# A two-layer decoder trunk on one core: four low parts moved to VectorE, one PSUM tile under another tag, one square root earlier in GpSimd's queue

## The chip, the core and the metric

The kernel runs on one core of a Trainium2 chip. The core has a matrix engine (TensorE; PE in the profile, with its weight loads as PEld), a vector engine (VectorE, DVE), a scalar engine (ScalarE, ACT), a general engine (GpSimd, POOL) and a queue that issues transfers (SyncE, SP). Each engine works through its own queue in order, and waits at an instruction whose inputs are not there. The metric is the time of one execution on the device in microseconds (us); lower is better. A profile is one further execution, recorded by the hardware profiler.

## What is computed

The reference takes x (512 positions by 1024 features, float32) through two layers. Cut to what matters:

```
for l in range(2):
    h = rms_norm(x, norm_mix_g[l])
    proj = h @ w_in[l]                 # attention | short convolution | RWKV-7
    ...
    x = x + mixed @ w_out[l]
    h = rms_norm(x, norm_mlp_g[l])
    x = x + square(relu(h @ w_mlp_up[l])) @ w_mlp_down[l]
return rms_norm(x, final_norm_g)
```

The change touches the last two lines of the loop, the MLP: 1024 features go up to 4096 and down again to 1024.

## The kernel before

Everything is kept transposed: a tile has 128 features on the partitions and the 512 positions along the row. x is eight such tiles (`x[0]` to `x[7]`). Each matrix product is made in near-full float32 precision from three passes. Every operand is split into a high part, which is its cast to a reduced format (made by ACT), and a low part, which is the operand less the high part (one subtraction on DVE or POOL). PE then adds up high by high, high by low and low by high. In the profile the parts of a weight are `whi` and `wlo`, those of a middle tile (a squared tile of the MLP) `mh` and `ml`, and those of the normalised input `ahif` and `alof`.

One layer has two stages.

- The **mixing stage** runs from the norm to the output projection, and also makes the first three of the MLP's up products (`NUP = 3`). Its order is written out by hand: the string `ORDER[l]` names work generators by letter, a number repeats a step, and `drive` (L225) takes the next step of each generator in that order. So the string sets the order of each engine's queue. The letters that matter here are d (loads), w (casts of a weight), x and y (low parts of a weight, x on DVE, y on POOL), m (one matmul of a product) and N (the steps of the MLP's norm).
- The norm before the MLP (`inner_norm`, L755) has five N steps: the sums of squares on PE (`pssf`), a scaling on DVE (`rsx`, L365), the inverse square root as a power on POOL (`rrf`, L369), its broadcast by PE (`prbf`), and a copy to `rs` by ACT (`rsf`, L771). In the last line of `ORDER[1]` the first N stands early. The scaling, the root and the broadcast follow at the end, with four m between them, and one y ahead of them.
- The **MLP stage** (from L1377) has no such string: the framework orders its instructions, and so they do not stand on an engine in the order of the code. `up(i)` finishes middle tile i for i from 0 to 3: `square` (L1397) multiplies the relu of the product by `rs` on DVE (L1402) and squares it on ACT (L1404); `kept` (L1388) makes the two parts, the high part on ACT (L1393), the low part on POOL (L1394). The other 28 middle tiles come in 14 pairs (`two`, L1451), each from seven products of 256 columns (`pa`, `pb`, `pc`, weights `shi_p` and `slo_p`). These use blocks that `by_gain` and `blocks` make on ACT and DVE beforehand (`bn`, `t`, `thi`, `tlo`).
- `down(h, js)` (L1521) multiplies four middle tiles by four of the eight output tiles and adds each to `x[j]` on DVE (L1540). The first call, `down(0, range(4))`, is special: outputs 0 and 1 are open at once, each with middle tiles 0 to 2 first, and then each with middle tile 3; their additions are L1535. Outputs 2 and 3 follow.

PSUM has eight banks here: four under the tag `rp`, two under `mm`, two under `at`. A tag's banks are used in turn, and a bank can be written again when its last reader is done. Outputs of `down` use `mm`. In the MLP stage `at` holds only `pc`. The first two up products stand in `mm`, the third and the fourth in `rp`.

Of the kernel before, what the change touches and what calls it, by code (L numbers as in the profile page):

```python
# [10 lines left out]
F32 = mybir.dt.float32  # L11
# [5 lines left out]
ALU = mybir.AluOpType  # L17
# [85 lines left out]

SLOTS = (
         "cp/rk 010 "
# [163 lines left out]
def tile_trunk(ctx: ExitStack, tc: tile.TileContext, xT, wts, prm_d, cst_d, lora_d, gup_d, lam_d, fin_d, out):  # L269
    nc = tc.nc  # L270
    act, dve, pool = nc.scalar, nc.vector, nc.gpsimd
# [27 lines left out]
    def psum(tag, bufs, name):  # L299
        return ps.tile([P, 512], F32, tag=tag, bufs=bufs, name=name)  # L300
# [4 lines left out]
    x = [cp.tile([P, S], F32, tag=f"x{j}", name=f"x{j}") for j in range(NK)]  # L305
# [23 lines left out]
    def weights(g, k0=0, k1=NK, home=None):  # L329

        for a in range(k0, k1, 4):
            n = min(4, k1 - a)
            turn[0] += 1
            if home is None and spare[0] and turn[0] % (WB + 1) == 0:
                pool_, tags, bufs = spare[0], ("raw4", "whi4", "wlo4"), 1
            else:
                pool_, tags, bufs = wp, ("raw", "whi", "wlo"), WB
            raw = pool_.tile([P, 4, P], F32, tag=tags[0], bufs=bufs, name=f"raw{g}_{a}")
            nc.sync.dma_start(raw[:, :n].rearrange("p k c -> p (k c)"), wts[g, :, a * P:(a + n) * P])
            if home is None:  # L340
                hi, lo = [pool_.tile([P, 4, P], F32R, tag=t, bufs=bufs, name=f"w{p}{g}_{a}") for p, t in zip(("hi", "lo"), tags[1:])]
            else:
                hi, lo = home(a)
            act.copy(hi[:, :n], raw[:, :n])  # L344
            (pool if a and lean[0] else dve).tensor_tensor(lo[:, :n], raw[:, :n], hi[:, :n].bitcast(F32), ALU.subtract)  # L345
            for k in range(n):
                yield hi[:, k], lo[:, k]
# [9 lines left out]
    def mm3(out_ps, w, acts, n=NK):  # L357
        for _ in mm3_steps(out_ps, w, acts, n):
            pass
# [12 lines left out]
    def norm_tile(j, key):  # L372

        if j == 0:
            acc = wp.tile([P, S], F32, tag="acc", bufs=1, name=f"acc{key}")
            nrm[key] = [acc]
            act.activation(acc, x[j], AF.Square)
        else:
            sq = wp.tile([P, S], F32, tag="sq", bufs=2, name=f"sq{key}_{j}")
            act.activation(sq, x[j], AF.Square)  # L380
            dve.tensor_tensor(nrm[key][0], nrm[key][0], sq, ALU.add)
# [187 lines left out]
    for l in range(L):  # L569
# [809 lines left out]
        with ExitStack() as mx:  # L1379
# [8 lines left out]
            def kept(m):  # L1388

                i = len(mids)  # L1390
                hi = fp.tile([P, S], F32R, tag="mh", bufs=RING, name=f"mh{l}_{i}")
                lo = fp.tile([P, S], F32R, tag="ml", bufs=RING, name=f"ml{l}_{i}")
                act.copy(hi, m)  # L1393
                pool.tensor_tensor(lo, m, hi.bitcast(F32), ALU.subtract)  # L1394
                mids.append((hi, lo))

            def square(cs, name):  # L1397

                r = fp.tile([P, S], F32, tag="r", bufs=2, name=f"r{name}")
                for i, c in enumerate(cs):  # L1400
                    q = slice(i * H, i * H + c.shape[1])
                    dve.scalar_tensor_tensor(r[:, q], c, 0.0, rs[:, q], ALU.max, ALU.mult)  # L1402
                m = fp.tile([P, S], F32, tag="m", bufs=3, name=f"m{name}")
                act.activation(m, r, AF.Square)  # L1404
                kept(m)
# [115 lines left out]
            def down(h, js):  # L1521

                g, k0 = h // 2, 4 * (h % 2)
                if h == 0 and js[0] == 0:
                    pts = [psum("mm", 2, f"dn{l}_{h}_{j}") for j in js[:2]]
                    ws = [list(weights(wbase + NG_IN + NG_OUT + NG_UP + 8 * g + j, k0, k0 + 4)) for j in js[:2]]
                    for a, b in ((0, 3), (3, 4)):
                        for j, pt, w in zip(js, pts, ws):
                            for k in range(a, b):
                                (whi, wlo), (ahi, alo) = w[k], mids[k]  # L1530
                                pe.matmul(pt, whi, ahi, start=(k == 0), stop=False)
                                pe.matmul(pt, whi, alo, start=False, stop=False)
                                pe.matmul(pt, wlo, ahi, start=False, stop=(k == 3))
                    for j, pt in zip(js, pts):
                        dve.tensor_tensor(x[j], pt, x[j], ALU.add)  # L1535
                    js = js[2:]
                for j in js:
                    pt = psum("mm", 2, f"dn{l}_{h}_{j}")
                    mm3(pt, weights(wbase + NG_IN + NG_OUT + NG_UP + 8 * g + j, k0, k0 + 4), mids[4 * h:4 * h + 4], 4)
                    dve.tensor_tensor(x[j], pt, x[j], ALU.add)  # L1540
                    if h == 2 * N_KG - 1 and j < NK - LATE:
                        norm_tile(j, f"m{l + 1}")
# [4 lines left out]
            for j in range(NK):  # L1547
                by_gain(j)
            down(0, range(4))
            for q in range(4):  # L1550
                blocks(q)
            h, half = 0, 1
            for p in range(N_TWO):
                two(N_ONE + p, N_ONE + N_TWO + p)
                if len(mids) >= 4 * h + 6 and h < 2 * N_KG - 2 * (l == L - 1):
                    down(h, range(4 * half, 4 * half + 4))
                    h, half = h + half, 1 - half
            while h < 2 * N_KG - 2 * (l == L - 1):
                down(h, range(4 * half, 4 * half + 4))
                h, half = h + half, 1 - half  # L1560
# [70 lines left out]
```

## Time and profile before

| | us |
|---|---|
| median of 3 runs | 1250.81 (1249.91 to 1251.99) |
| the profiled execution's own time | 1245.9 |
| its span, first to last instruction | 1244.1 |
| first middle tile's multiplication by rs (L1402) starts, layer 0 | at 290.31 |
| the same, layer 1 | at 901.73 |

The profile gives for each engine the time in which it was busy, lists the instructions in order of time with the idle time before each and what ended it, and sums up who waited for whom. The matrix engine's granted clock was 0.998 of full speed over the span. A time such as 307.22 is counted from the span's start.

### The profile page before, as it was taken

How to read it: one execution, taken by the hardware profiler on the slowest of the kernel's cores; microseconds unless marked ns; L12 is line 12 of the kernel's file. 1: busy time of each engine (PE TensorE's matmuls, PEld its weight loads, DVE VectorE, ACT ScalarE, POOL GpSimd, SP SyncE). 2: the span in 40 equal slices, each digit the busy share in tenths (PEclk: the TensorE clock that was granted, in tenths of full speed). 3: DMA queues.
4: the chain of work that ended last, by engine and by line, in shares of the span. 5: the costliest groups of instructions: out<-in, count | busy, mean ns of one | idle time of the engine just before them, and what ended most of it. 6: DMA issues, size and time to landing. Idle time of an engine off the chain costs nothing.

```text
span 1244.1 us, 25538 instructions
## 1 busy us (share of the span) xinstructions
PE 1228.2 (99%) x9716; PEld 1055.9 (85%) x9716; DVE 931.8 (75%) x1796; ACT 693.0 (56%) x1462; POOL 363.6 (29%) x457
## 2 busy tenths in 40 slices
PE   9999999999999999999999999999999999999997
PEld 6788788887899898989888888888779999998987
DVE  6787888869887676765666777887798867676753
ACT  6785655648455454544465657564675545454552
POOL 1264637343121112120035455463221211111111
PEclk9999999999999999999999999999999999999999
DMA  6523333142432333321235233332433333323121
GB/s 216 164 90 95 113 88 110 52 161 77 136 102 94 106 99 102 100 87 44 68 105 164 82 118 117 94 83 75 150 104 109 107 105 95 109 94 105 57 69 68
DMA packets 84698, 127.94 MB, mean 103 GB/s; under 512 B 21472, under 2 KB 25568, under 8 KB 84576
## 3 DMA queue, kind: packets, MB, share of 16 engines
q1 hardware_dynamic: 83568, 125.64, 32.7%
q8 instruction: 76, 1.25, 0.4%
q10 hardware_dynamic: 1008, 0.68, 0.2%
q14 instruction: 46, 0.38, 0.1%
HBM read 117.11 MB, written 9.18 MB: 102 GB/s over the span
## 4 chain that ended last, share of the span: by engine, by line
PE 93%; DVE 3%; ACT 2%; DMA 1%; issue 1%; POOL 0%; POOLq 0%; SPq 0%; ACTq 0%; DVEq 0%
PE dn L282 24%; PE pj L282 22%; PE pa L282 13%; PE po L282 8%; PE pb L282 7%; PE dnF L282 4%; PE pc L282 3%; PE up L282 3%; PE sc L282 1%; PE ptt L287 1%; PE pg L282 1%; PE pyy L282 1%; DVE tlo L1449 1%; PE pzw L282 1%; PE pst L282 1%
## 5 line engine op out<-in xcount | busy, mean ns | idle before, releaser
L1394 POOL TENSOR_TENSOR ml<-m,mh 128x512 fp32r<-128x512 f32 x64 | 104.5, 1649 | 489.1 <-ACT mh L1393 348.0
L282 PE MATMUL dn<-mh,whi 128*128 128x512 f32 x448 | 175.8, 392 | 2.1 <-DVE x L1535 2.1
L282 PE MATMUL dn<-ml,whi 128*128 128x512 f32 x448 | 175.3, 391 | 2.0 <-POOL ml L1394 2.0
L282 PE MATMUL dn<-mh,wlo 128*128 128x512 f32 x448 | 175.2, 391 | 0.0
L683 POOL TENSOR_TENSOR wlo<-raw,whi 128x512 fp32r<-128x512 f32 x84 | 111.2, 1324 | 211.5 <-ACT whi L671 169.6
L344 ACT CAST whi<-raw 128x512 fp32r<-128x512 f32 x126 | 77.7, 618 | 157.9 <-PE dn L282 148.1
L282 PE MATMUL pj<-ahim,whi 128*128 128x512 f32 x392 | 156.7, 400 | 0.4 <-DVE vf L1280 0.4
L282 PE MATMUL pj<-ahim,wlo 128*128 128x512 f32 x392 | 156.4, 399 | 0.0
L282 PE MATMUL pj<-alom,whi 128*128 128x512 f32 x392 | 155.9, 398 | 0.0
L1540 DVE TENSOR_TENSOR x<-dn,x 128x512 f32<-128x512 f32 x108 | 74.5, 690 | 91.5 <-PE dn L282 91.3
L671 ACT CAST whi<-raw 128x512 fp32r<-128x512 f32 x142 | 87.7, 617 | 76.4 <-PE pj L282 28.9
L1463 ACT CAST shi_p<-s 128x512 fp32r<-128x512 f32 x112 | 69.5, 621 | 79.6 <-PE pa L282 62.3
L345 DVE TENSOR_TENSOR wlo<-raw,whi 128x512 fp32r<-128x512 f32 x126 | 100.2, 797 | 10.2 <-ACT whi L344 7.4
L282 PEld LDWEIGHTS dn<-ml,whi 128*128 128x128 f32 x448 | 84.2, 188 | 19.8 <-POOL ml L1394 2.8
L282 PEld LDWEIGHTS dn<-mh,whi 128*128 128x128 f32 x448 | 84.1, 188 | 20.0 <-DVE x L1535 2.5
L282 PEld LDWEIGHTS dn<-mh,wlo 128*128 128x128 f32 x448 | 84.2, 188 | 18.5
L282 PE MATMUL pa<-thi,shi_p 128*128 128x256 f32 x336 | 95.2, 283 | 0.1
L282 PE MATMUL pa<-tlo,shi_p 128*128 128x256 f32 x336 | 94.9, 282 | 0.0
L282 PE MATMUL pa<-thi,slo_p 128*128 128x256 f32 x336 | 94.2, 280 | 0.0
L1464 DVE TENSOR_TENSOR slo_p<-s,shi_p 128x512 fp32r<-128x512 f32 x112 | 77.7, 695 | 21.8 <-ACT shi_p L1463 19.0
L282 PEld LDWEIGHTS pj<-ahim,whi 128*128 128x128 f32 x392 | 73.8, 188 | 14.0 <-issue 0.8
L282 PEld LDWEIGHTS pj<-alom,whi 128*128 128x128 f32 x392 | 73.9, 188 | 13.9 <-issue 0.5
(416 smaller groups left out, 3246.2 us busy)
## 6 DMA issues: line engine op xcount, KB each, us to landing
raw<-wts SPq DMA_DIRECT2D x389, 256.0 KB, 2.6
qs<-dqhi SPq DMA_DIRECT2D x24, 128.0 KB, 3.5
ks<-dkhi SPq DMA_DIRECT2D x24, 128.0 KB, 3.3
x<-xT SPq DMA_DIRECT2D x8, 256.0 KB, 5.9
dqhi<-qhi SPq DMA_DIRECT2D x6, 256.0 KB, 3.6
dqlo<-qlo SPq DMA_DIRECT2D x6, 256.0 KB, 3.6
dkhi<-khi SPq DMA_DIRECT2D x6, 256.0 KB, 3.0
dklo<-klo SPq DMA_DIRECT2D x6, 256.0 KB, 3.4
```

What stands on the lines that cost most here:

```text
L282: ins = nc.tensor.matmul(*a, **k)
L287: ins = nc.tensor.transpose(*a, **k)
L344: act.copy(hi[:, :n], raw[:, :n])
L345: (pool if a and lean[0] else dve).tensor_tensor(lo[:, :n], raw[:, :n], hi[:, :n].bitcast(F32), ALU.subtract)
L671: yield act.copy(hi[:, k0:k1], raw[:, k0:k1])
L683: yield eng.tensor_tensor(lo[:, k0:k1], raw[:, k0:k1], hi[:, k0:k1].bitcast(F32), ALU.subtract)
L1394: pool.tensor_tensor(lo, m, hi.bitcast(F32), ALU.subtract)
L1449: dve.tensor_tensor(lo[:, u], t, hi[:, u].bitcast(F32), ALU.subtract)
L1463: act.copy(hi, src)
L1464: dve.tensor_tensor(lo, src, hi.bitcast(F32), ALU.subtract)
L1540: dve.tensor_tensor(x[j], pt, x[j], ALU.add)
```

## The change

Three edits.

1. In `kept`, the low parts of the middle tiles 0 to 3 are made by DVE, those of the other 28 by POOL as before. This holds for both layers.
2. In the first call of `down`, output 0 gets its PSUM tile under the tag `at`, output 1 under `mm`. Before, both had `mm`. With the turn of the two `mm` banks, output 2 then follows on the bank that output 1 doesn't have, and output 3 on that of output 1.
3. In the last line of `ORDER[1]`, the y (a low part of a weight on POOL) goes behind the scaling and the root, which now stand together (`m4 N2 y m8 N` in place of `y m4 N m4 N m4 N`). The number of matmuls between the first of these steps and the broadcast is the same. Layer 0's string is not changed.

```diff
-... m5 x m w y m4 N m4 N m4 N m2 w y m N m33 ")
+... m5 x m w m4 N2 y m8 N m2 w y m N m33 ")
```

```diff
                 act.copy(hi, m)
-                pool.tensor_tensor(lo, m, hi.bitcast(F32), ALU.subtract)
+                (dve if i < 4 else pool).tensor_tensor(lo, m, hi.bitcast(F32), ALU.subtract)
                 mids.append((hi, lo))
```

```diff
                 if h == 0 and js[0] == 0:
-                    pts = [psum("mm", 2, f"dn{l}_{h}_{j}") for j in js[:2]]
+                    pts = [psum(("at", "mm")[j], 2, f"dn{l}_{h}_{j}") for j in js[:2]]
```

2 rows, old and new, of the table ORDER are left out of this document.

## The prediction

> **What bounds the kernel now.** I read the page's head first, then the list of what TensorE (PE) waits for, then the order of time around each wait.
>
> ```profile
> span 1244.1 us, 25538 instructions
> PE 1228.2 (99%) x9716; PEld 1055.9 (85%) x9716; DVE 931.8 (75%) x1796; ACT 693.0 (56%) x1462; POOL 363.6 (29%) x457
> PE dn L282 <- DVE x L1535: 2.1, 2, 1.2
> PE dn L282 <- POOL ml L1394: 2.0, 2, 1.0
> PE prbf L282 <- POOL rrf L369: 0.6, 1, 0.6
> ```
>
> PE is busy for 99% of the span, so the kernel gets faster only where PE stops waiting. The last three rows are from the list of PE's waits (total us, times, longest). They are the waits which the three edits name: the low part of a middle tile (ml), the addition that empties a down bank (x, L1535), and layer 1's root (rrf). Together 4.7 us. What each costs in the order of time is a little more, because PE restarts slowly (columns: start, us, engine, line):
>
> ```profile
> 307.22 0.39 PE L282 MATMUL dn<-mh,whi 128*128 128x512 f32 x1
> 308.65 0.50 PE L282 MATMUL dn<-ml,whi 128*128 128x512 f32 x1 [1.04 <-POOL ml L1394]
> 308.99 0.40 PE L282 MATMUL dn<-mh,wlo 128*128 128x512 f32 x1
> 309.23 0.39 PE L282 MATMUL dn<-mh,whi 128*128 128x512 f32 x1
> ```
>
> and a little later, for the addition,
>
> ```profile
> 310.51 0.27 PE L282 MATMUL pa<-ahif,slo_p 128*128 128x256 f32 x1
> 311.94 0.50 PE L282 MATMUL dn<-mh,whi 128*128 128x512 f32 x1 [1.16 <-DVE x L1535]
> ```
>
> and the same two in layer 1:
>
> ```profile
> 915.90 0.39 PE L282 MATMUL dn<-mh,whi 128*128 128x512 f32 x1
> 917.20 0.50 PE L282 MATMUL dn<-ml,whi 128*128 128x512 f32 x1 [0.92 <-POOL ml L1394]
> ...
> 921.34 0.28 PE L282 MATMUL pa<-alof,shi_p 128*128 128x256 f32 x1
> 922.60 0.50 PE L282 MATMUL dn<-mh,whi 128*128 128x512 f32 x1 [0.99 <-DVE x L1535]
> ```
>
> A 512-column matmul normally follows the one before by 0.23 us (308.99 to 309.23), a 256-column one by 0.12. Layer 0, first wait: 308.65 - 307.22 = 1.43, less 0.23 is 1.20; the step after it (308.65 to 308.99) takes 0.34, 0.11 too much: **1.31**. The other three restart with the same 0.50 matmul, so I add 0.11 to each. Second wait: 311.94 - 310.51 = 1.43, - 0.12 + 0.11 = **1.42**. Layer 1 in the same way: 1.30 - 0.23 + 0.11 = **1.18** and 1.26 - 0.12 + 0.11 = **1.25**. The root:
>
> ```profile
> 898.95 0.39 PE L282 MATMUL up<-ahif,wlo 128*128 128x512 f32 x1
> 899.91 1.16 PE L282 MATMUL prbf<-cst,rrf 128*128 128x128 f32 x8 [0.57 <-POOL rrf L369]
> ```
>
> 899.91 - 898.95 - 0.23 = 0.73, and I put the restart at 0.10 here too: **0.83**. All five: 1.31 + 1.42 + 1.18 + 1.25 + 0.83 = 5.99 us. That is what there is to win.
>
> **Root ahead of the weight's low part (layer 1).** One instruction changes place in POOL's queue; nothing is added.
>
> ```profile
> 896.22 0.15 DVE L365 TENSOR_SCALAR rsx<-pssf 128x4 f32<-128x4 f32 x1
> ...
> 897.13 1.30 POOL L683 TENSOR_TENSOR wlo<-raw,whi 128x512 fp32r<-128x512 f32 x1 [7.01 <-ACT whi L671]
> 898.39 1.47 POOL L369 TENSOR_TENSOR rrf<-rsx,ones 128x4 f32<-128x4 f32 x1
> ```
>
> The root's input is there at 896.37, and POOL was idle for 7 us before 897.13. With the root first it runs from 896.4 to 897.9; PE asks for it at 899.18. So the 0.83 goes whole (if the power stretches to twice 1.47, it still ends in time). Behind the root waits the weight's low part: it would end near 899.2 instead of 898.43. It belongs to the third up tile, whose first matmul comes 12 matmuls after prbf, near 903. Cost nothing.
>
> **Low parts on DVE.** Per layer four POOL instructions go and four DVE instructions come. A DVE subtraction of this shape takes 0.68 us (299.13 below); two in an unbroken row take 1.27 (311.21), so each needs 0.60 of the queue. In order of time, all three engines, layer 0's low parts 0 and 1:
>
> ```profile
> 294.52 0.84 DVE L345 TENSOR_TENSOR wlo<-raw,whi 128x512 fp32r<-128x512 f32 x1 [1.11 <-ACT whi L344]
> 295.09 1.43 POOL L1394 TENSOR_TENSOR ml<-m,mh 128x512 fp32r<-128x512 f32 x1 [0.27 <-ACT mh L1393]
> 295.57 1.50 DVE L345 TENSOR_TENSOR wlo<-raw,whi 128x512 fp32r<-128x512 f32 x1 [0.20 <-ACT whi L344]
> ...
> 299.13 0.68 DVE L345 TENSOR_TENSOR wlo<-raw,whi 128x512 fp32r<-128x512 f32 x1
> ```
>
> then low parts 2 and 3 and the additions:
>
> ```profile
> 300.98 2.80 POOL L1394 TENSOR_TENSOR ml<-m,mh 128x512 fp32r<-128x512 f32 x1 [4.46 <-ACT mh L1393]
> 302.55 1.77 DVE L1449 TENSOR_TENSOR tlo<-t,thi 128x512 fp32r<-128x512 f32 x1
> ...
> 306.36 0.62 ACT L1393 CAST mh<-m 128x512 fp32r<-128x512 f32 x1
> 306.72 2.16 DVE L1446 TENSOR_TENSOR t<-bn,t 128x256 f32<-128x256 f32 x3
> 307.05 1.54 POOL L1394 TENSOR_TENSOR ml<-m,mh 128x512 fp32r<-128x512 f32 x1 [3.27 <-ACT mh L1393]
> ...
> 311.21 1.27 DVE L1535 TENSOR_TENSOR x<-dn,x 128x512 f32<-128x512 f32 x2
> ```
>
> and layer 1:
>
> ```profile
> 906.75 1.58 DVE L345 TENSOR_TENSOR wlo<-raw,whi 128x512 fp32r<-128x512 f32 x1 [1.86 <-PE up L282]
> ...
> 911.75 1.28 ACT L474 ACT_TABLE_LOAD   x1
> ...
> 913.84 3.31 POOL L1394 TENSOR_TENSOR ml<-m,mh 128x512 fp32r<-128x512 f32 x1 [6.07 <-ACT mh L1393]
> ...
> 916.54 1.16 DVE L345 TENSOR_TENSOR wlo<-raw,whi 128x512 fp32r<-128x512 f32 x1
> 917.76 0.61 ACT L1393 CAST mh<-m 128x512 fp32r<-128x512 f32 x1
> 918.23 2.52 DVE L1446 TENSOR_TENSOR t<-bn,t 128x256 f32<-128x256 f32 x4
> 918.45 1.34 POOL L1394 TENSOR_TENSOR ml<-m,mh 128x512 fp32r<-128x512 f32 x1 [1.30 <-ACT mh L1393]
> ...
> 921.87 1.28 DVE L1535 TENSOR_TENSOR x<-dn,x 128x512 f32<-128x512 f32 x2
> ```
>
> The important thing here is that a POOL low part already costs DVE time. The DVE subtraction of 295.57 takes 1.50 instead of 0.68 and ends at 297.07, 0.55 after POOL's; that of 302.55 takes 1.77 and ends at 304.32, 0.54 after POOL's 303.78. DVE stands still until POOL is done. [...]
>
> Layer 0's stretch where DVE has no gap (busy for 5.00 in the 5 us from 305, last fence of this text): what goes is 1.77 - 0.68 = 1.09, and about 1.1 from the three steps of 306.72 (2.16, where three of 0.41, less the overlap of 0.08, take 1.07); what comes is two low parts, 1.20. DVE is about 1.0 earlier at the x additions. Low parts 0 and 1 fall where DVE has gaps (1.11 before 294.52, 1.86 before 906.75). Layer 1: the four steps of 918.23 lose about 1.1 (2.52 against 1.4) and the weight's low part of 916.54 loses 0.5, less 1.20: 0.4 earlier, and up to 0.8 more because the root lets the stage begin sooner.
>
> What is late next is low part 3. Layer 0: its cast ends at 306.98, DVE at the earliest at 307.7, PE asks at 307.45: 0.3 late plus 0.1 to restart, if nothing upstream moves; the square behind it is 0.5 earlier on DVE (1.09 less one low part), so I take 0.1, bounds 0 and 1.0 (one more DVE instruction ahead of it). Layer 1: without the wait at 917.20, PE asks 13 steps after 915.90, at 918.86; cast end 918.37 plus 0.75 is 919.12; and PE is up to 0.8 further ahead. I take 0.5, bounds 0 and 1.3. Low part 2 there has its cast just before 913.84, so it is ready near 914.6; PE asks at 916.1. How DVE's queue is ordered is not in the trace, since the framework sets it; hence the wide bounds.
>
> **First down output in another bank.** No instruction is added. Output 2 no longer waits for the addition of output 0: of its bank, the other one of the tag mm, the last reader was the square of an up tile, which the low parts 0 and 1 stand behind already. The next dependence is output 3 on the addition of output 1. Layer 0: outputs 0 and 1 end three steps after 309.23, at 309.92, less 1.31 is 308.61, output 2 takes twelve steps (2.73), to 311.34. The two additions end now at 311.21 + 1.27 = 312.48; 1.0 earlier is 311.5: 0.2 late. Layer 1: near 922.4 against 923.15 less 0.4 to 1.2. I take 0.4 for both layers, bounds 0 and 2.2 (no DVE gain). The six pa matmuls that filled the gap run later, the same work.
>
> **The sum.** 5.99 - 0.1 - 0.5 - 0.4 = 5.0 us. The profiled execution took 1245.9 us (span 1244.1 and 1.8 around it): 1240.9. The median of the runs, 1250.81, stands 4.9 above it; I carry the difference over: **1245.8**. With all bounds against it (4.5) 1.5 us are left, with all in favour 6.0; I take 3.0 to 6.0, so 1244.8 to 1247.8, as the forecast's own range. Does the won time last? PE has no other wait to speak of until the end, and DVE catches up:
>
> ```profile
> 305.00:310.00 5.00, 3.96 (x18) 2.89 (x17) 5.00 (x8) 3.28 (x7) 1.54 (x1) 1.00 0.16 52
> ...
> 330.00:335.00 5.00, 5.00 (x23) 4.05 (x22) 3.37 (x5) 0.87 (x2) 3.22 (x2) 1.00 0.42 145
> ```
>
> (PE, weight load, DVE, ACT, POOL busy in 5 us.) From 330 DVE has gaps again, so PE coming 2 to 3 us earlier finds its operands.
>
> **Rivals.** *The waits move* (14%): DVE's queue is what sets these waits, and with the low parts in it the low parts and the additions come just as late. The wait of output 2 turns up at output 3, and low part 3 is late by most of a full wait in both layers: the root and a quarter of the other four are won, 0.83 + 5.16 / 4 = 2.1: 1248.7. For it: DVE has no gap there. Against: the 1.0 worked out above. [...]
>
> *The order differs* (7%): a low part stands in DVE's queue ahead of its cast and holds squares and additions up. Layer 1's low part 2 is the place: ACT puts a table load of 1.28 (911.75) before its cast, which an order made beforehand may not count. A hold costs PE about as much as the load, and then again in what DVE does next; with one such hold in each wait's place, 4 x 1.28 = 5.1, nothing of the 5.0 is left but noise: about 1250.5.
>
> *Slower* (9%): in the pair stage DVE becomes the bound. A new order puts one instruction ahead of the low part (slo_p) that the next product needs, in each of the 28 pairs. At half an instruction, 0.34, it costs 9.5: 1250.8 - 5.0 + 9.5 = 1255.3; it decides from (5.0 + 2.5) / 28 = 0.27 a pair. For it: DVE takes on work. Against: the list of PE's waits has no row for slo_p, and DVE has gaps from 330.
>
> *It doesn't do what it says* (2%): the framework's order on PE and DVE keeps the same matmuls waiting, 1250.8.
>
> **How the numbers follow.** The forecast has 68%. About 0.2%, 2.5 us, is what a measurement of this kernel can tell from no change, so faster ends at 1248.3: the forecast and the better third of the moved waits, 0.68 + 0.04 = 0.72. Slower is the one case, 0.09; the rest is 0.19. The range runs from 1244.0 (all five won, and 0.8 for the spread of the runs) to 1250.0; it leaves out the slower case, no change, and most of the differing order, together 0.16.
>
> **What would show it.** DVE has 8 instructions more, POOL 8 fewer; L1394 on POOL counts 56. PE's wait for rrf is gone. PE's wait for L1535 is gone or stands at output 3 and is below 0.5. A wait for ml names DVE and is below 0.5 a layer. DVE's long subtractions beside POOL (1.50, 1.77) are 0.68. Wrong is it if PE shows a wait for slo_p in the pair stage, or if output 3 waits for a microsecond.

## The result, and the profile after

| | before | after |
|---|---|---|
| median of 6 runs, us | 1250.27 (1248.29 to 1251.99) | 1239.68 (1239.49 to 1240.52) |
| profiled execution, us (its span) | 1245.9 (1244.1) | 1239.57 (1237.8) |

The ratio of the times is 0.9918 (0.9906 to 0.9931): 10.6 us faster, where 5.0 were forecast, and below the range. From one profiled execution to the other it is 6.3 us. The two differences do not agree, and the experiments are about that.

First what the profile of the changed kernel says. The head of its page and the top of the list of PE's waits:

```profile
span 1237.8 us, 25529 instructions
PE 1226.2 (99%) x9716; PEld 1055.3 (85%) x9716; DVE 932.3 (75%) x1804; ACT 692.3 (56%) x1462; POOL 350.2 (28%) x449
```

```profile
PE idle L282 <- DVE zero L394: 1.2, 1, 1.2
PE prbF L282 <- ACT rhiF L509: 0.8, 1, 0.8
```

DVE has its 8 instructions more and POOL its 8 fewer. DVE is busy for only 0.5 us longer (931.8 before), though 8 x 0.68 = 5.4 us of work came to it: its subtractions no longer stand behind POOL's. Beside low parts 0 to 2 of layer 0, where two of them took 1.50 and 1.77 us before, each takes 0.68 or 0.69 now. The list has no row for dn and none for prbf: all five waits that the prediction added up are gone. The order of time in layer 0, at the same place as the prediction's rows:

```profile
306.31 0.69 DVE L1394 TENSOR_TENSOR ml<-m,mh 128x512 fp32r<-128x512 f32 x1
...
307.24 0.40 PE L282 MATMUL dn<-mh,whi 128*128 128x512 f32 x1
...
307.47 0.40 PE L282 MATMUL dn<-ml,whi 128*128 128x512 f32 x1
...
308.40 0.40 PE L282 MATMUL dn<-mh,wlo 128*128 128x512 f32 x1
...
308.52 1.28 DVE L1535 TENSOR_TENSOR x<-dn,x 128x512 f32<-128x512 f32 x2
308.63 0.40 PE L282 MATMUL dn<-mh,whi 128*128 128x512 f32 x1
```

Low part 3 is ready at 307.00, and PE asks for it at 307.47. Output 2 follows on output 1 at the normal step of 0.23 (308.40 to 308.63). The two additions start at 308.52 instead of 311.21. Two stretches of 30 us, layer 0 and layer 1, after and then before (the stretch, then busy time of PE, weight load, DVE, ACT, POOL, then PE's granted clock):

```profile
290.00:320.00 30.00, 30.00 (x157) 25.71 (x156) 28.52 (x52) 21.90 (x41) 1.19 (x1) 1.00 0.32 100
900.00:930.00 30.00, 30.00 (x167) 26.24 (x166) 28.80 (x53) 22.00 (x42) 0.00 (x0) 1.00 0.38 116
```

```profile
290.00:320.00 30.00, 27.80 (x134) 22.98 (x133) 27.80 (x46) 20.75 (x38) 8.25 (x5) 1.00 0.30 95
900.00:930.00 30.00, 28.10 (x134) 23.20 (x135) 26.07 (x44) 22.07 (x40) 8.52 (x5) 1.00 0.28 87
```

PE was idle for 2.20 and 1.90 us there, and now is not idle at all. So in these two executions the gain is where the prediction put it. The root in layer 1:

```profile
893.66 1.02 POOL L369 TENSOR_TENSOR rrf<-rsx,ones 128x4 f32<-128x4 f32 x1 [6.32 <-DVE none L1420]
894.65 1.66 POOL L683 TENSOR_TENSOR wlo<-raw,whi 128x512 fp32r<-128x512 f32 x1
...
896.37 1.05 PE L282 MATMUL prbf<-cst,rrf 128*128 128x128 f32 x8
```

It is ready 1.7 us before PE wants it. What is left to explain is the other 4 us.

### The profile page after: what moved, and what is told of

Its sections match the earlier page's. It is cut to its first block, busy times and chain, and to the rows that moved or that the text cites. A ratio compares the mean times of both kernels' runs of the same rounds, so it can differ in the third digit from the quotient of the medians.

```text
span 1237.8 us, 25529 instructions
## 1 busy us (share of the span) xinstructions
PE 1226.2 (99%) x9716; PEld 1055.3 (85%) x9716; DVE 932.3 (75%) x1804; ACT 692.3 (56%) x1462; POOL 350.2 (28%) x449
## 3 DMA queue, kind: packets, MB, share of 16 engines
q8 instruction: 76, 1.25, 0.4%
## 4 chain that ended last, share of the span: by engine, by line
PE 94%; ACT 2%; DVE 2%; POOL 1%; DMA 1%; issue 1%; ACTq 0%; POOLq 0%; DVEq 0%
PE dn L282 25%; PE pj L282 21%; PE pa L282 13%; PE po L282 8%; PE pb L282 7%; PE dnF L282 4%; PE pc L282 3%; PE up L282 3%; PE sc L282 1%; PE ptt L287 1%; PE pg L282 1%; PE pyy L282 1%; DMA raw<-wts 1%; PE pzw L282 1%; PE pst L282 1%
## 5 line engine op out<-in xcount | busy, mean ns | idle before, releaser
L1394 POOL TENSOR_TENSOR ml<-m,mh 128x512 fp32r<-128x512 f32 x56 | 91.1, 1645 | 496.2 <-ACT mh L1393 337.6
```

The lines of the kernel that those rows point to most:

```text
L1394: (dve if i < 4 else pool).tensor_tensor(lo, m, hi.bitcast(F32), ALU.subtract)
```

## The experiments

The theory after this result: the profiled execution of before is not the usual one, and in the usual one something near these five waits is longer. Rival: the change wins about 5 us at the five places and some 4 us more elsewhere, or the edits help each other in some other way.

**The kernel before once more**, with its own profile. No edit.

> The kernel before once more, for a second profile and its spread. Its timed runs had a median of 1250.3 us (1248.3 to 1252.0), its first profiled execution only 1245.9; the changed kernel 1239.7 (1239.5 to 1240.5), profiled 1239.6. The waits worked out at 5.99 us explain the 6.3 between the two profiles, not the further 4.3 of the medians. Theory A (the 4.3 sits in the low parts on GpSimd, which shut out VectorE or are shut out by it for a time that differs from run to run): about 1250, spread 2 to 4 us, and a second profile that is longer than 1246 has its extra time in the waits for ml and in the DVE work around them. Theory B (it sits in the bank wait), theory C (in the root's wait): the extra time stands in front of output 2, or of prbf. Theory D (elsewhere): in none of these.

Measured: 1249.06 us, ratio 1.0002 (0.9992 to 1.0013). This time the profiled execution took 1249.83 us. Its page, its list of PE's waits and its order of time in layer 0:

```profile
span 1248.0 us, 25538 instructions
```

```profile
PE dn L282 <- POOL ml L1394: 4.7, 2, 3.7
...
PE dn L282 <- DVE x L1535: 1.0, 1, 1.0
```

```profile
293.09 1.29 POOL L1394 TENSOR_TENSOR ml<-m,mh 128x512 fp32r<-128x512 f32 x1 [2.34 <-ACT mh L1393]
...
306.29 1.08 DVE L1446 TENSOR_TENSOR t<-bn,t 128x256 f32<-128x256 f32 x3
...
306.62 4.28 POOL L1394 TENSOR_TENSOR ml<-m,mh 128x512 fp32r<-128x512 f32 x1 [3.28 <-ACT mh L1393]
306.82 0.40 PE L282 MATMUL dn<-mh,whi 128*128 128x512 f32 x1
307.30 0.68 DVE L1464 TENSOR_TENSOR slo_p<-raw,shi_p 128x512 fp32r<-128x512 f32 x1
307.90 1.28 DVE L1449 TENSOR_TENSOR tlo<-t,thi 128x512 fp32r<-128x512 f32 x2
...
309.11 0.68 DVE L1464 TENSOR_TENSOR slo_p<-s,shi_p 128x512 fp32r<-128x512 f32 x1
310.96 0.79 PE L282 MATMUL dn<-ml,whi 128*128 128x512 f32 x1 [3.74 <-POOL ml L1394]
311.55 0.63 PE L282 MATMUL dn<-mh,wlo 128*128 128x512 f32 x1
...
312.22 0.69 DVE L1535 TENSOR_TENSOR x<-dn,x 128x512 f32<-128x512 f32 x1 [2.43 <-PE dn L282]
...
316.67 0.57 PE L282 MATMUL dn<-mh,wlo 128*128 128x512 f32 x1
317.07 0.39 PE L282 MATMUL dn<-mh,whi 128*128 128x512 f32 x1
317.30 0.40 PE L282 MATMUL dn<-ml,whi 128*128 128x512 f32 x1
```

This is the same program as in the prediction, and the same instruction, low part 3 of layer 0, takes 4.28 us on POOL instead of 1.54. Low part 0, the first row, takes 1.29. In the prediction's execution DVE was the one held up (its three steps took 2.16 us). Here they take 1.08: DVE goes through an unbroken row of seven instructions with two inputs each, to 309.79, and POOL ends only at 310.90, 1.11 us after that row. PE waits for 3.74 us, and then its matmuls last 0.63 and follow each other by 0.43 us, not by 0.23, until about 317. The windows of one microsecond give the granted clock (third number from the right, ahead of DMA share and GB/s):

```profile
310.00:311.00 1.00, 0.04 (x1) 0.04 (x1) 0.00 (x0) 0.00 (x0) 0.91 (x1) 0.60 0.00 0
...
317.00:318.00 1.00, 1.00 (x6) 0.76 (x6) 0.00 (x0) 0.00 (x0) 0.00 (x0) 0.99 0.77 246
```

Between these rows it is 0.50. A mean of 0.60 in one microsecond is half speed for (1 - 0.60) / 0.5 = 0.80 of it, so the half clock runs from 310.20 to 317.02.

The price in layer 0: the wait costs 310.96 - 306.82 - 0.23 = 3.91; from 310.96 to 317.30 stand 12 steps of 0.23 and 6 of 0.12 (matmuls of 512 and of 256 columns), 3.48 us, which took 6.34: 2.86 more. Together 6.8 us, where the prediction's execution lost 1.31 + 1.42 = 2.73 in this layer (there is no wait for the addition in layer 0 now, since the other one hides it). The difference of 4.0 is that of the spans, 1248.0 - 1244.1 = 3.9. Of 78 timed runs of before in the four sets of experiments, this kernel's among them, 7 are below 1246.2, and their medians lie from 1248.87 to 1249.29. So, by its time, the execution of the first profile was a rare one (7 of 78). The profiles of two kernels below that also leave low part 3 on POOL (without the low parts, and the bank alone) show the long form as well: 4.28 us on POOL and a wait of 3.79 and 3.77.

**The change with one edit left out.** In the same set:

```diff
# without the low parts: edits 2 and 3 only
-                (dve if i < 4 else pool).tensor_tensor(lo, m, hi.bitcast(F32), ALU.subtract)
+                pool.tensor_tensor(lo, m, hi.bitcast(F32), ALU.subtract)
# without the bank: edits 1 and 3 only
-                    pts = [psum(("at", "mm")[j], 2, f"dn{l}_{h}_{j}") for j in js[:2]]
+                    pts = [psum("mm", 2, f"dn{l}_{h}_{j}") for j in js[:2]]
# without the root: edits 1 and 2 only
-... m5 x m w m4 N2 y m8 N m2 w y m N m33
+... m5 x m w y m4 N m4 N m4 N m2 w y m N m33
```

> Bank and root edits, low parts of the first four middle tiles back on GpSimd. Theory A: the two waits for ml return (1.31 + 1.18) and the 4.3 with them: 1239.7 + 2.5 + 4.3 = 1246.5, spread over 2 us. Theories B, C and D: 1239.7 + 2.5 = 1242.2, spread about 1 us.

> Low parts and root edits, both first down outputs under the tag mm again. Theory B: 1239.7 + 2.7 + 4.3 = 1246.7. The others: the two waits of output 2 return, 1.42 + 1.25: 1242.4; with theory A the spread stays at 1 us.

> Low parts and bank edits, layer 1's root behind the weight's low part again. Theory C: 1239.7 + 0.8 + 4.3 = 1244.8. The others: 1239.7 + 0.83 = 1240.5, spread about 1 us.

| edits | us | ratio to before | PE's waits for dn and prbf |
|---|---|---|---|
| bank, root | 1247.64 | 0.9991 (0.9982 to 1.0) | ml from POOL 3.79 and 0.98, x 0.4 |
| low parts, root | 1239.5 | 0.9921 (0.9908 to 0.9935) | none |
| low parts, bank | 1240.28 | 0.9929 (0.9917 to 0.9942) | prbf 0.6 |

Without the low parts nearly nothing is won; theory A had 1246.5, so 1.1 less than was measured. Without the bank nothing is lost, although every theory had 2.7 us to lose there (1242.4), so all of them missed this: the six pa matmuls stand ahead of output 2 again and fill 0.7 us, and the additions are done in time:

```profile
308.19 1.28 DVE L1535 TENSOR_TENSOR x<-dn,x 128x512 f32<-128x512 f32 x2
```

Leaving the root out brings its wait of 0.6 back.

**One edit alone, and the low parts divided.**

```diff
# one low part: on the kernel before
-                pool.tensor_tensor(lo, m, hi.bitcast(F32), ALU.subtract)
+                (dve if i == 3 and l == 0 else pool).tensor_tensor(lo, m, hi.bitcast(F32), ALU.subtract)
# low parts 0 to 2: on the kernel before
-                pool.tensor_tensor(lo, m, hi.bitcast(F32), ALU.subtract)
+                (dve if i < 3 else pool).tensor_tensor(lo, m, hi.bitcast(F32), ALU.subtract)
```

> The low parts on VectorE and nothing else of the change. The second profile of the kernel before showed low part 3 of layer 0 taking 4.28 us on GpSimd, PE waiting 3.74 for it and running at half clock behind it. Theory A': that wait (3.91 with the lost step), the slow matmuls behind it (2.9), layer 1's two waits (1.18 + 1.25) all go with the low parts alone, 9.2 us: about 0.8 behind the changed kernel for the root, 1240.3, spread 1 us. Rival: the bank edit is needed in one of the layers, and 1.3 to 2.7 us more are lost: 1241.6 to 1243.

> The bank edit alone. Theory A': in most executions layer 0's PE waits for low part 3 so long that the additions are done anyway, so only layer 1's 1.25 can be won: 1 us under the kernel before (1248.9 on the last chip), spread over 2 us, profile with the long wait for ml. Rival: both waits of output 2 go, 2.7 us under.

> One instruction of the change: low part 3 of layer 0 on VectorE, all others on GpSimd. Theory A': the long wait and the slow clock of layer 0 go (6.8), layer 1's 1.18 + 1.25 + 0.83 stay, and perhaps a wait of output 2 in layer 0 (0 to 1.4): 5.4 to 6.8 under the kernel before, spread about 1 us. Rival (the loss is spread over all eight low parts): 1 to 2 us under.

> Low parts 0, 1 and 2 on VectorE in both layers, low part 3 on GpSimd. Theory A': low part 3 still meets VectorE's unbroken row in layer 0, PE still waits 3 us or more for it and the clock falls: the long loss stays, and only layer 1's 1.18 for low part 2 may go, or come back at low part 3; 0 to 2 us under the kernel before. Rival (spread over all): about three quarters of the 9 us, 6 to 7 under.

| on the kernel before | us | ratio to before |
|---|---|---|
| edit 1 alone | 1240.78 | 0.9938 (0.9926 to 0.995) |
| edit 2 alone | 1248.26 | 0.9996 (0.9987 to 1.0004) |
| low part 3 of layer 0 alone | 1244.72 | 0.9969 (0.9957 to 0.9981) |
| low parts 0 to 2 of both layers | 1246.21 | 0.9983 (0.9973 to 0.9992) |

Of these, the bank alone moves nothing that can be measured: in layer 0 low part 3 holds PE for 3.77 us first, and the additions of the first two outputs cost nothing more behind it. In layer 1 the wait for the addition does go; 1 us was expected for it, and the 0.5 us measured are inside the noise. One single subtraction, moved from POOL to DVE, wins 3.9 us (2.4 to 5.4). That is below the 5.4 to 6.8 that were expected. Part of the gap is seen: in layer 0 PE now waits 0.5 us for the addition of an output and 0.2 for a slo_p. The rest is that the 6.8 came from one execution: at the same place the bank alone loses 5.6 us (3.94 for the wait, 1.68 for the slow matmuls). PE's waits in the kernel with the one subtraction moved:

```profile
PE dn L282 <- DVE x L1535: 1.5, 2, 1.0
...
PE dn L282 <- POOL ml L1394: 0.9, 1, 0.9
...
PE prbf L282 <- POOL rrf L369: 0.6, 1, 0.6
...
PE dn L282 <- DVE ml L1394: 0.2, 1, 0.2
```

The wait of 3.7 is 0.2, the clock stays at 1.00 in layer 0, and what is left are waits that are gone in the changed kernel. The two profiles differ by more (1248.0 - 1241.8 = 6.2), because this execution of before lies 0.8 above its median and this one of the new kernel 1.1 below its own.

Moving the other low parts wins 2.1 us, where the theory had 0 to 2 and its rival 6 to 7. With the low parts 0 to 2 moved and low part 3 left on POOL, POOL takes 3.49 and 3.33 us for it in the two layers, and PE waits for it in both. The profiled execution, 1248.53 us, was the slowest of this kernel's twelve, so it need not be the usual one:

```profile
309.39 0.50 PE L282 MATMUL dn<-ml,whi 128*128 128x512 f32 x1 [2.14 <-POOL ml L1394]
309.73 0.39 PE L282 MATMUL dn<-mh,wlo 128*128 128x512 f32 x1
...
310.94 0.42 PE L282 MATMUL pa<-ahif,slo_p 128*128 128x256 f32 x1
...
921.79 0.80 PE L282 MATMUL dn<-ml,whi 128*128 128x512 f32 x1 [1.97 <-POOL ml L1394]
```

```profile
309.00:310.00 1.00, 0.61 (x3) 0.52 (x4) 0.00 (x0) 0.07 (x1) 0.33 (x1) 1.00 0.00 0
310.00:311.00 1.00, 1.00 (x7) 0.87 (x6) 0.84 (x2) 0.93 (x2) 0.00 (x0) 0.90 0.00 0
...
314.00:315.00 1.00, 1.00 (x6) 0.83 (x5) 0.01 (x1) 0.00 (x0) 0.00 (x0) 0.89 0.03 4
...
921.00:922.00 1.00, 0.21 (x1) 0.21 (x2) 0.00 (x0) 0.00 (x0) 0.74 (x1) 0.89 0.00 0
...
1239.00:1240.00 1.00, 0.81 (x4) 0.81 (x5) 0.59 (x4) 0.13 (x1) 0.00 (x0) 0.61 0.74 260
```

Here PE first runs at full speed for 1.4 us after the wait, and only then at half clock, from 310.80 to 314.22: 3.42 us. That is half of the 6.82 us above. In layer 1 it begins at 921.78, and at the end of the kernel, where PE runs out of work, once more at 1239.22.

**Is it the wait that halves the clock, or POOL's work?** Two kernels on the changed one made low part 3 of layer 0 later without POOL, by doing its subtraction four or eight times on DVE with the same result.

```diff
-                (dve if i < 4 else pool).tensor_tensor(lo, m, hi.bitcast(F32), ALU.subtract)
+                [(dve if i < 4 else pool).tensor_tensor(lo, m, hi.bitcast(F32), ALU.subtract) for _ in range(4 if i == 3 and l == 0 else 1)]
```

> The changed kernel with the subtraction of layer 0's low part 3 made four times over on VectorE (the same result each time): it ends 1.8 us later, and PE, which had 0.45 to spare, waits about 1.4. If a wait costs its length: 1239.7 + 1.5 = 1241.2, and the granted clock stays at 1.0 behind it.

> The same with eight subtractions, 4.2 us later: PE waits about 3.8, as it did in the second profile of the kernel before. If a long wait costs its length alone: 1239.7 + 3.9 = 1243.6. If it also brings the half clock seen there (2.9 us in the slow matmuls): 1246.5, with the clock near 0.5 for about 5 us behind the wait. This kernel has no GpSimd low part there, so the slow clock would be the wait's doing and not GpSimd's.

Measured: 1239.31 us, ratio 0.9927 (0.9906 to 0.9947), and 1242.93, 0.9956 (0.9941 to 0.9971). Both tell nothing on the question. The framework put pair products into the gap: with four, PE waits nowhere near it; with eight, for 0.5 us at a slo_p and, 37 us later, for 1.5 at pa, and the clock stays 1.00. That profile is of the fastest of the five executions. In three of the other four the mean granted clock is 0.996 instead of 0.998, so a half clock may have come there; they left no trace. In this stage PE's order was not held fixed while one operand came late. The stage with the order written out by hand does hold it. One of its last steps is the root on POOL, here made four or seven times over with the same result each time (the cut shows four):

```diff
-        yield pool.tensor_tensor(y, xx, mhalf.to_broadcast([P, n]), ALU.pow)
+        yield [pool.tensor_tensor(y, xx, mhalf.to_broadcast([P, n]), ALU.pow) for _ in range(times)][-1]
...
-                yield from root_steps(r, pt[:, :NB], NB)
+                yield from root_steps(r, pt[:, :NB], NB, times=4 if l == 1 else 1)
```

> The changed kernel, with layer 1's root power on POOL issued four times with the same result, in the stage whose order is written out by hand, so that PE has nothing to put into the gap. The root begins at 893.7 and takes 1.02; four end near 897.8, and PE asks at 896.4: PE waits about 1.4 us at prbf, and pays 0.1 of restart. Theory (only a wait of about 2 us or more halves the clock): 1.5 us slower than the changed kernel, near 1241.1, matmuls after prbf at their normal step of 0.23, granted clock 1.00 up to 905. Rival A (any wait above 1 us halves the clock): some 2 to 3 us more, near 1244. Rival B (POOL's low part, not PE's wait, goes with the half clock): near 1241.1 here too. Rival C (the wait is taken up later by slack): near 1239.7.

> The same with seven powers: they end near 900.9, PE waits about 4.4 us at prbf. The low part of a weight behind the root on POOL ends near 902.2, and PE asks for it 3.8 us after prbf, near 904.7: it hides. Theory (a long wait of PE by itself brings the half clock): the wait of 4.4 plus 2.5 to 3 us of matmuls at a step of 0.43 instead of 0.23, near 1239.7 + 7.2 = 1246.9, granted clock near 0.5 for 4 to 5 us behind the wait. Rival B (the half clock comes from something else in that place of layer 0): 4.5 us slower, near 1244.2, step 0.23 and clock 1.00. Rival C (slack): below 1242.

Measured: 1241.95 us, ratio 0.9938 (0.9919 to 0.9957), with four powers, and 1247.0, 0.9985 (0.9972 to 0.9997), with seven. Four powers, order of time and windows:

```profile
892.85 4.77 POOL L369 TENSOR_TENSOR rrf<-rsx,ones 128x4 f32<-128x4 f32 x4 [6.32 <-DVE none L1420]
...
895.33 0.39 PE L282 MATMUL up<-ahif,wlo 128*128 128x512 f32 x1
897.68 1.56 PE L282 MATMUL prbf<-cst,rrf 128*128 128x128 f32 x8 [1.96 <-POOL rrf L369]
...
899.46 0.63 PE L282 MATMUL up<-alof,whi 128*128 128x512 f32 x1
```

```profile
898.00:899.00 1.00, 1.00 (x9) 1.00 (x7) 0.00 (x0) 0.00 (x0) 1.00 (x2) 0.64 0.00 0
...
901.00:902.00 1.00, 1.00 (x4) 0.76 (x4) 0.46 (x2) 1.00 (x3) 0.00 (x0) 0.65 0.63 166
```

and seven:

```profile
895.47 0.39 PE L282 MATMUL up<-ahif,wlo 128*128 128x512 f32 x1
901.07 2.08 PE L282 MATMUL prbf<-cst,rrf 128*128 128x128 f32 x8 [5.21 <-POOL rrf L369]
...
903.37 0.63 PE L282 MATMUL up<-alof,whi 128*128 128x512 f32 x1
```

```profile
900.00:901.00 1.00, 0.00 (x0) 0.00 (x0) 0.00 (x0) 0.00 (x0) 0.99 (x2) 0.94 0.00 0
...
904.00:905.00 1.00, 1.00 (x5) 0.77 (x5) 0.92 (x2) 1.00 (x2) 0.00 (x0) 0.85 0.66 168
```

The half clock is there in both, with no low part of the MLP on POOL near it and in another stage: the wait of PE brings it, not the low part. POOL is at work on the powers during these waits, but work on POOL alone does not halve the clock: in the changed kernel POOL is busy for 4.88 of the 5 us from 738, with PE busy throughout and a clock of 1.00. The half clock runs from 898.28 to 901.70 and from 900.88 to 904.30, 3.42 us each time. The price with four powers: 897.68 - 895.33 - 0.23 = 2.12 for the wait. The ninth matmul after prbf comes 4.43 us behind it instead of 2.74, so 1.69 for the clock; 3.81 in all, of which 0.81 goes because this execution reached the root 0.81 earlier than the one of the changed kernel. 3.0 is left, which is the difference of the spans (1240.8 - 1237.8). By the medians it is 2.3 (1241.95 - 1239.68), so not every execution need have paid it in full. With seven: 5.37 + 1.61 - 0.67 = 6.3, again the difference of the spans (1244.1 - 1237.8). The median with seven, 1247.0, is the 1246.9 that was expected, but that is in part luck: the wait was 1 us longer than the 4.4 put down for it, and the slow matmuls cost 1.6 where 2.5 to 3 were put down.

The size of the first was missed: the powers take 1.19 us each in a row, not 1.02, so the wait grew to 1.96 where 1.4 was meant, and that already halved the clock in the profiled execution. By the expectation's own bound (about 2 us) it stands at the edge. Waits of 1.04 and 1.16 (the first profile of before) and of 1.5 (eight subtractions) did not halve it. No kernel was made to find the border between 1.5 and 1.96; the last section has what the traces show of it.

## Why the prediction was wrong

**What bounds the kernel** was the right list of places, taken from an unusual execution. The five waits are gone, as the prediction said, and the spans of the two first profiles confirm the size: 6.3 us against 5.99 for all five.

**The failed step** is in the sum: "The median of the runs, 1250.81, stands 4.9 above it; I carry the difference over". Those 4.9 us were not spread over the kernel. 4.0 of them are the same wait for low part 3 of layer 0, in its usual, longer form with the half clock behind it, and they went with it. The row that could have warned is in the prediction: DVE's three steps of 2.16 us, held up by POOL, whose low part had got in first. A page of one execution shows one outcome; in the second profile the three steps took 1.08 us and POOL was the one held up (4.28). By terms: the layer 0 low part was put at 1.31 and the wait on the addition behind it at 1.42, together 2.73; in the second profile this place costs 6.8 (and 5.6 with the bank alone). With the other three terms (1.18 + 1.25 + 0.83) the execution of the second profile loses 10.1 us here, and the spans differ by 1248.0 - 1237.8 = 10.2. Of the 6.1 us between the forecast (1245.8) and the measured 1239.68, this step is 4.9; the three amounts held back, 0.1 + 0.5 + 0.4, are another 1.0. A median far above the profiled execution should have been a case of its own with a chance, 1250.8 - 10 = 1240.8.

**Root ahead of the low part:** 0.83 forecast. Leaving it out brings back a wait of 0.6 (0.9929 against 0.9918, with intervals that overlap). The wait's going is shown by the profile; its size is too small for the times.

**Low parts on DVE:** that a low part on POOL holds DVE up was right (1.50 and 1.77 us where a subtraction by itself takes 0.68), but at the place that counts the prediction had the direction wrong. It let DVE get back about 1.1 us from its three steps; in the second profile these take 1.08 already, POOL was the one held up, and PE paid for it. At low part 2 the direction was right in both profiles (DVE's subtraction of 1.77). The edit carries most of the gain: edit 1 alone 0.9938 where the whole change has 0.9918, edits 2 and 3 without it 0.9991. What edits 2 and 3 add to it, 1.1 us by the medians (1240.78 and 1239.68, from different sets), is not clear of the noise. The 0.1 and 0.5 held back for a late low part 3 were not needed. In layer 0 its cast ends at 306.16 instead of 306.98, because the work ahead of it on DVE is earlier, and the framework put the subtraction ahead of the three t steps, not behind them.

**The bank** was credited with 1.42 + 1.25. Those two waits do go, but the earlier additions take them away: without the bank edit they are gone too (0.9921 against 0.9918), and with the bank edit alone nothing is won (0.9996). Two edits were aimed at the same delay, and the prediction gave each a share. The 0.4 held back for output 3 was nothing.

**Rivals.** The waits did not move: no row of PE's list has dn. The pair stage did not become bound by DVE: PE's list has no row for slo_p. One low part did stand ahead of its cast, but not the one that was named: low part 1 of layer 1 (902.84) held DVE for 0.87 us, and PE's list has no wait from it. Low part 2 there started at 909.95, behind its cast, which ended at 909.73. The moved work won 7.7 us by itself (0.0062 of 1249): at the places that cost time, one of the two engines had been held up by the other each time, POOL at low part 3 (4.28 us in the second profile) and DVE at low part 2 (1.77).

No kernel tried beats the changed one beyond the intervals. By these runs the bank edit could be dropped without loss.

## What to carry to other kernels

When the profiled execution is some microseconds faster or slower than the median, don't carry the difference over as a constant: profile the same kernel again and look for the wait that changed, first where two engines hold each other up. Price a wait of PE at its length only while it is short: here waits of 1.04, 1.16 and 1.5 us brought no half clock, and waits of 2.0 to 5.2 us cost 1.6 to 2.9 us more than their length, and the longest not the most (1.7 at 1.96 us, 1.7 and 2.9 at 3.8, 1.6 at 5.2). Two edits that each "remove a wait" share one gain if the same late engine is behind both; try each alone.

## What was not expected of the hardware

A subtraction on POOL can lose to a whole row of DVE instructions. Low part 3 began at 306.62, inside a row of DVE instructions with two inputs each, and ended 1.11 us after the last of the row, where low part 0 of the same execution took 1.29 in all. Four more low parts (without the low parts, the bank alone, and both layers with low parts 0 to 2 moved) end 1.12 us after such a row. In the prediction's execution DVE was the one that ended behind POOL, by 0.55 and 0.54 us, in the subtractions of 1.50 and 1.77. So each engine was seen held up by the other, and here POOL was behind not one instruction but all those that followed without a gap. Why POOL got in between two of them in the prediction's execution and not in the next is open: the two rows began at different moments against the cast, but nothing was tried that sets this moment.

The half clock comes in pieces. In the six profiles that show it before the end of the kernel it lasted 3.42 us or twice that: 3.42 in both layers with low parts 0 to 2 moved, with the bank alone, with four and with seven powers, 6.82 and 6.84 in the second profile of before and without the low parts; it began up to 1.4 us after the wait had ended (310.80 against 309.39), or before it had ended (900.88 against 901.07). Waits of 1.96, 1.97 and 2.14 us, well below the length of a piece, were enough for one; the longest wait without one was 1.5 (eight subtractions).

In three profiles the beginnings lie whole multiples of one length apart. With low parts 0 to 2 moved, the half clock begins at 310.80, 921.78 and 1239.22: 610.98 and 317.44 us apart. Counted in pieces of 3.42 us the nearest whole numbers are 179 and 93, and 610.98 / 179 and 317.44 / 93 both give 3.413. In the second profile of before (310.20 and 1242.04) and with four powers (898.28 and 1236.20) the distances are 931.84 and 337.92, which is 273 and 99 times this length. So the beginnings in an execution lie as if it were divided into stretches of 3.41 us. That is the author's reading of these four distances; no run was made to test it. By it, what counts is how a wait falls into these stretches, not its length alone. From 20 us to the last stage of the kernel, in all profiles kept, PE was idle for 1.95 us or more of the stretch just ahead of a half clock, and for at most 1.62 of any other stretch at full speed (seven powers, 894.05 to 897.47: that wait began there, and the clock halved only a whole stretch later). Between 1.62 and 1.95 nothing was measured, and in the last stage, whose matmuls are small, 1.52 us idle in the 3.41 ahead of the half clock (the first profile of before) and 1.58 (the changed kernel) were enough, so idle time is not the whole measure. The second piece came where the wait reached far into the first: 0.76 us in the second profile of before and 1.72 without the low parts, against 0.19 with seven powers, which has one piece. With the bank alone the wait had ended 0.71 us ahead of the half clock, and there is one piece too. So nearly the same wait cost 2.9 us more in one execution (3.74, two pieces) and 1.7 in the other (3.77, one piece).
